# Transfers issued by ScalarE, smaller rings, a moved bias table and norm sums, and 14 U steps through HBM in a one-core transformer layer

## The chip, the cores and the metric

The kernel runs on one core of a Trainium2 chip. The metric is device time in microseconds (us) from the start to the end of one execution. An execution is also profiled: the profile gives, for each engine, when each instruction ran and what it waited for. TensorE multiplies matrices, VectorE and ScalarE work on tiles in on-chip memory, GpSimd does simple vector work and issues the indirect row gathers, and SyncE issues transfers. Each engine works through its own list of instructions in order.

## The reference, cut to what matters

One layer of a streaming encoder over 640 rows of width 2048: 512 new prompt frames (four tiles of 128) and 128 sample frames (one tile).

```
def layer(x, ...):
    z = rmsnorm(x, norm_mix_g) @ w_in
    q, k, v, u, vs, ga, gb = split_in(z, sgu_norm_g)
    o = attend(q, k, v, rel_bias(table), mask, sinks)     # sliding window, grouped heads
    s = sgu(u, vs, w_s, b_s)                              # gated mixing over 128 frames
    h = x + merge(o, s, ga, gb, w_branch_attn, w_branch_sgu, w_out)
    return h + peer(rmsnorm(h, norm_ffn_g))

def peer_tokens(xt, w_query, sub_keys, expert_u, expert_v):
    s = einsum('thpd,hpnd->thpn', query(xt), sub_keys)    # 8 heads, 2 halves, 128 keys
    sv, si = top_k(s, 16);  cv, ci = top_k(all sums of pairs, 16)
    eidx = the 16 * 8 expert numbers of the token, out of 16384
    a = gelu(expert_u[eidx] . xt)
    return sum(softmax(cv) * a * expert_v[eidx])
```

The result is the layer's output after a last norm, with the new rows of K, V and of the gated branch.

## The kernel before

The tokens go through in two groups. G1 is tile 0 and the sample; G2 is tiles 1, 2 and 3. The order in time is: the input projections, attention and gated branch of G1 ("mix"), G1's query with the search for the best experts, the mix of G2, the query of G2, a weights stage, and then the dense experts.

All large products run in `gemm` (lines 192 to 218). It loads two rows of weight blocks (`raw`, 512 KB, a ring of 4), splits each block into a high half (`whi`, a ScalarE cast, line 143) and a low half (`wlo`, a subtraction, line 144, on VectorE), both in rings of 5, and issues three products per tile (lines 211 to 213). After each pair of blocks `pump` advances a list of side generators (`side`: attention, gated branch, search, lookups, one-hots) by a pace of `steps[0]`, and `tick` advances the background gather (`bg`).

The experts are applied in two ways. For G1 `gather_peer` fetches 128 rows of U and 128 of V per token by indirect DMA (two tiles, 512 steps of 1 MB), and VectorE does a dot product (line 740) or an accumulation (line 745) on each. For G2 all experts are computed densely. `weights` builds a 128 x 16384 matrix of gates for each tile from one-hots (lines 782 to 799) and writes it to HBM (`wd`). U step s (`U`, 32 of them) gives 512 activations per token through a gelu (line 829); the first LEAD of them go to HBM as `ad` (line 831), since the gates aren't there yet. `h_step` loads the gates (line 813), multiplies them by the activations (line 814), transposes the product (line 818) and splits it into HT, which `V` (16 blocks of four column parts) multiplies by the V weights and adds to y. `late` does the same for the steps whose activations went to HBM and loads them first. `LEAD` also says which blocks of V run before a U step: from block LEAD/2 - 1 on, the two U steps for the next block come between the parts of V.

`prep` brings the input tiles: x pieces of four blocks, times the norm's gain, split into halves; then the sums of squares, for which ScalarE reads xn (line 435). For G1 it runs in the start, driven by `start_rows`; for G2 it is a side generator `nextg`, eight steps of which `first` lets run in the second branch of the mix of G1, four more in G1's query, and the rest behind those. `bias_table` (lines 222 to 233) computes a table of relative position biases and writes it to HBM (`bvd`), from where the attention loads it. `sample_consts` (lines 312 to 332) loads the caches for the sample.

What sets the order: the kernel's code is a Python program that emits instructions; a scheduler then places each on its engine's list by readiness and priority, so an edit moves instructions far from it. Each transfer that SyncE or ScalarE issues is counted by one of eight counters, taken in turn, and it waits until the counter's previous transfer has landed. SyncE issues nearly all transfers, GpSimd the gathers.

The lines that the prediction's steps touch:

```
    w = load(wd[G[i]][:, s * 512:s * 512 + 512])          # 813, SyncE
    nc.vector.tensor_mul(w, w, a)                          # 814
    ...
    nc.sync.dma_start(ad[s][i], a)                         # 831, SyncE
    ...
    x1 = load(x1d[i][:, nb * 512:nb * 512 + 512])          # V, b == 0
    nc.vector.tensor_add(y[i, nb], x1, ps)                 # 847
```

Of the kernel before, what the change touches and what calls it, by code (L numbers as in the profile page):

```python
# [18 lines left out]
D = 2048  # L19
KC = 16  # L20
# [5 lines left out]
LEAD = 12  # L26
RATE_A = 1.35
# [5 lines left out]
SW = 1.6  # L33
# [9 lines left out]
D_STAGE = 5  # L43
D_LOAD = 4
# [15 lines left out]
def body(tc, A, O):  # L60
    nc = tc.nc
    with ExitStack() as ctx:
# [34 lines left out]
        def load(src, shape=(128, 512)):  # L97
            t = pools["wk"].tile(list(shape), F32, name=nm("b"), tag="b", bufs=cfg["b"])
            nc.sync.dma_start(t, src)
            return t  # L100
# [211 lines left out]
        def sample_consts(vnat, out):  # L312
            vnd = dr.tile([128, 128], F32, name="vnd")
            nc.sync.dma_start(vnd, vnat)
            yield
            kc = mtile([128, 2, 8, 128])
            nc.vector.memset(kc, 0.0)
            for kv in range(2):
                nc.sync.dma_start(kc[kv * 64:kv * 64 + 64, kv], A["kcT"][kv * 64:kv * 64 + 64])
            vc = mtile([128, 8, 128])  # L320
            nc.sync.dma_start(vc, A["vc"])
            sk = stat(2)
            nc.sync.dma_start(sk, A["sinks_s"])
# [5 lines left out]
            vn = mtile([16, 8, 128])  # L329
            nc.sync.dma_start(vn, vnd.rearrange("(b t) d -> t b d", b=8))  # L330
            out.extend((kc, vc, vn, sk, bias))
            yield
# [86 lines left out]
        def prep(G, xgT, r1, order):  # L419
            for i, c in order:  # L420
                if c == 0:
                    xgT.append((mtile([128, KC, 128], F32R), mtile([128, KC, 128], F32R)))
                xh, xl = xgT[i]
                k = slice(4 * c, 4 * c + 4)
                x = stage((128, 4, 128))
                nc.sync.dma_start(x, A["xT"][G[i]][:, k, :])
                (nc.vector if len(G) == 2 and c + i == 0 else nc.gpsimd).tensor_mul(
                    x, x, gmix[:, k].unsqueeze(2).to_broadcast([128, 4, 128]))
                split(xh[:, k, :], xl[:, k, :], x)
                yield  # L430
            for i, ti in enumerate(G):
                s4 = stat(5)
                for c in range(4):
                    xn = load(A["xn"][ti][:, c * 512:c * 512 + 512])
                    nc.scalar.activation(xn, xn, AF.Square, accum_out=s4[:, c:c + 1])
                nc.vector.tensor_reduce(s4[:, 4:5], s4[:, 0:4], axis=AX.X, op=ALU.add)
                r1.append(rstd(s4[:, 4:5], D, "r1"))
                yield
# [4 lines left out]
        def mix(G, xgT, r1, ticks, pre=None):  # L443
# [90 lines left out]
            if n == 2:  # L534
                side.append(first(nextg, EARLY))
# [239 lines left out]
        def weights(ti, ijg):  # L775
# [7 lines left out]
            for t0 in range(0, 128, 4):  # L783
# [15 lines left out]
                nc.sync.dma_start(wd[ti][t0:t0 + 4, :].rearrange("t (i j) -> i t j", i=128), w)  # L799
                yield  # L800

        def dense_peer(G, x2T, r2, x1d):
            n = len(G)
            ad = [[dr.tile([128, 512], F32, name=nm("ad")) for _ in G] for _ in range(LEAD)]
            if True:
# [3 lines left out]
                def h_step(s, i, a):  # L809
                    b, hf = divmod(s, 2)  # L810
                    if (b, i) not in HT:
                        HT[b, i] = mtile([128, 2, 8, 128], F32R)
                    w = load(wd[G[i]][:, s * 512:s * 512 + 512])
                    nc.vector.tensor_mul(w, w, a)  # L814
                    yield
# [19 lines left out]

                def late(s):
                    for i in range(n):
                        a = load(ad[s][i])
                        yield from h_step(s, i, a)

                def V(b, nb, ticks):
                    def ev(i, ps):
                        x1 = y.get((i, nb))
                        if b == 0:
                            x1 = load(x1d[i][:, nb * 512:nb * 512 + 512])
                            y[i, nb] = slot()
                        nc.vector.tensor_add(y[i, nb], x1, ps)  # L847
                        if b == 15:
# [8 lines left out]
                gf = {}  # L857
                steps[0] = SW
# [9 lines left out]
                open_work("d")  # L868
                steps[0] = 1.0
# [30 lines left out]
        side.append(bias_table())  # L900

        def start_rows(kc):
# [3 lines left out]
            if kc == 6:  # L906
                side.insert(0, start)
# [106 lines left out]
```

## Time and profile before

| what | value |
|---|---|
| median of 3 runs | 3991.54 us (3985.18 to 3993.43) |
| the profiled execution | 3996.57 us, of which the span of instructions 3994.9 us |
| TensorE busy | 3883.8 us, 97% |
| VectorE busy | 3153.5 us, 79% |
| ScalarE busy | 1728.2 us, 43% |
| GpSimd busy | 829.1 us, 21% |
| moved by DMA | 1180.5 MB, 296 GB/s in the mean |

The shares are averages over stages with different limits; which wait counts is read from each stage. The stages by time: mix of G1 to 562 us, its query to about 700, mix of G2 to 1510, its query to 1757, the weights stage to 2206, the dense experts to 3976, then the last norm. In the trace a row names the line, the engine and the tiles (out<-in); the time in brackets is how long the engine was idle before, with what released it. PE is TensorE, PEld its weight loads, DVE VectorE, ACT ScalarE, POOL GpSimd, SP SyncE. The clock is the share of full speed that TensorE was granted; full speed is 2.4 GHz and 0.50 is 1.2 GHz. Lines are those of the kernel before.

### The profile page before, as it was taken

What the parts mean: (1) busy time and instruction counts of PE and PEld (TensorE: products, weight loads), DVE (VectorE), ACT (ScalarE), POOL (GpSimd) and SP (SyncE); (2) the same over time, 40 slices, a digit from 0 to 9 for tenths busy, and PEclk for the clock granted to TensorE, in tenths of its full rate; (3) what the DMA queues carried; (4) which work ended last, traced back from release to release, by engine and by line L of the source; (5) the groups of instructions that cost most, each with busy time, mean ns of one, the idle gap of its engine ahead of it and who ended that gap; (6) DMA issues with size and microseconds to landing.
All of it is one profiled execution on the core that took longest, in us unless ns stands there. A gap on an engine that the chain in (4) does not pass through costs nothing. (4 is left out here: it accounts for less than half of the span.)

```text
span 3994.9 us, 52665 instructions
## 1 busy us (share of the span) xinstructions
PE 3883.8 (97%) x17880; PEld 3177.5 (80%) x17880; DVE 3153.5 (79%) x5421; ACT 1728.2 (43%) x3338; POOL 829.1 (21%) x678
## 2 busy tenths in 40 slices
PE   8999998999999999999999899999999999999998
PEld 6778786877777888877878788877888888888886
DVE  4655769966767987899977688878888888888888
ACT  5665554444444334436665333333333333333333
POOL 1000113211212223211111112222222222222222
PEclk9999999999999999999999999999999999999999
DMA  7666786777878997569988989989998999999987
GB/s 224 204 187 208 248 264 201 273 276 279 311 277 286 336 334 249 206 198 314 327 264 288 338 325 338 342 299 365 338 350 336 353 331 345 345 340 349 346 337 290
DMA packets 333919, 1180.51 MB, mean 296 GB/s; under 512 B 35840, under 2 KB 94784, under 8 KB 267088
## 3 DMA queue, kind: packets, MB, share of 16 engines
q1 hardware_dynamic: 259824, 640.15, 47.9%
q0 software_dynamic: 73824, 536.99, 35.0%
q8 instruction: 141, 2.31, 0.2%
q14 instruction: 130, 1.06, 0.1%
HBM read 1117.69 MB, written 59.31 MB: 295 GB/s over the span
## 5 line engine op out<-in xcount | busy, mean ns | idle before, releaser
L211 PE MATMUL acc<-whi,m 128*128 128x512 f32 (+1 forms) x5232 | 2066.7, 395 | 23.3 <-ACT whi L143 18.3
L212 PE MATMUL acc<-wlo,m 128*128 128x512 f32 (+1 forms) x5232 | 2049.8, 392 | 22.5 <-DVE wlo L144 22.4
L213 PE MATMUL acc<-whi,m 128*128 128x512 f32 (+1 forms) x5232 | 2044.1, 391 | 0.3 <-DVE m L144 0.2
L143 ACT CAST whi<-raw 128x512 fp32r<-128x512 f32 (+1 forms) x1888 | 1157.9, 617 | 1979.3 <-PE acc L213 1646.6
L144 DVE TENSOR_TENSOR wlo<-raw,whi 128x512 fp32r<-128x512 f32 (+1 forms) x1824 | 1221.5, 689 | 526.8 <-ACT whi L143 523.1
L212 PEld LDWEIGHTS acc<-wlo,m 128*128 128x128 f32 x5232 | 990.7, 189 | 227.1 <-DVE wlo L144 34.5
L211 PEld LDWEIGHTS acc<-whi,m 128*128 128x128 f32 x5232 | 989.3, 189 | 225.4 <-ACT whi L143 20.6
L213 PEld LDWEIGHTS acc<-whi,m 128*128 128x128 f32 x5232 | 989.5, 189 | 202.7 <-DVE m L144 0.8
L740 DVE SCALAR_TENSOR_TENSOR gb<-gb,xa 128x2048 f32<-128x2048 f32 x256 | 589.6, 2303 | 79.5 <-DMA gb<-in_U,idx 69.1
L745 DVE SCALAR_TENSOR_TENSOR xa<-gb,hw,xa 128x2048 f32<-128x2048 f32 x239 | 560.3, 2344 | 70.4 <-DMA gb<-in_V,idx 64.1
L754 POOL DMA_INDIRECT gb<-in_V,idx x239 | 318.5, 1333 | 1228.8 <-DVE wlo L144 331.2
L754 POOL DMA_INDIRECT gb<-in_U,idx x256 | 339.6, 1327 | 1018.9 <-ACT whi L143 366.2
L144 POOL TENSOR_TENSOR wlo<-raw,whi 128x512 fp32r<-128x512 f32 x64 | 91.5, 1431 | 261.8 <-ACT whi L143 229.7
L796 PEld LDWEIGHTS pm<-s 128*128 128x128 f32 x768 | 102.6, 193 | 30.5 <-ACT s L793 14.6
L796 PE MATMUL pm<-s 128*128 128x128 f32 x768 | 113.7, 283 | 10.0 <-DVE s L789 8.0
L789 DVE TENSOR_SCALAR s<-io,S 128x128 f32<-128x128 f32 x384 | 114.8, 339 | 3.6 <-DMA wd<-s 3.6
L847 DVE TENSOR_TENSOR s<-s,acc 128x512 f32<-128x512 f32 x180 | 112.5, 678 | 0.0
L144 DVE TENSOR_TENSOR m<-pm,m 128x512 fp32r<-128x512 f32 (+1 forms) x142 | 93.5, 661 | 7.5 <-ACT m L143 6.5
L143 ACT CAST m<-pm 128x512 fp32r<-128x512 f32 (+1 forms) x142 | 79.6, 563 | 16.3 <-PE pm L362 6.3
L798 ACT COPY s<-pm 128x512 f32<-128x512 f32 x96 | 56.5, 588 | 64.8 <-PE pm L796 64.2
L814 DVE TENSOR_TENSOR b<-b,b 128x512 f32<-128x512 f32 x36 | 24.8, 688 | 56.0 <-DMA b<-wd 53.5
L792 ACT ACTIVATE s<-io,S 128x128 f32<-128x128 f32 x192 | 66.7, 398 | 3.6 <-DVE S L782 2.3
(194 smaller groups left out, 1668.7 us busy)
## 6 DMA issues: line engine op xcount, KB each, us to landing
raw<-in_UT SPq DMA_DIRECT2D x256, 512.0 KB, 6.2
raw<-in_VP SPq DMA_DIRECT2D x256, 512.0 KB, 6.5
raw<-in_w_in SPq DMA_DIRECT2D x224, 512.0 KB, 4.6
raw<-in_w_out SPq DMA_DIRECT2D x64, 512.0 KB, 5.4
raw<-in_w_q SPq DMA_DIRECT2D x64, 512.0 KB, 4.5
wd<-s SPq DMA_DIRECT2D x96, 256.0 KB, 6.0
b<-wd SPq DMA_DIRECT2D x96, 256.0 KB, 5.2
raw<-in_w_pa SPq DMA_DIRECT2D x32, 512.0 KB, 4.2
```

Of the source, the lines that this page charges most:

```text
L143: mark[0] = nc.scalar.copy(hi, src).ins
L144: (E or nc.vector).tensor_sub(lo, src, hi.bitcast(F32))
L211: nc.tensor.matmul(o, xh, hi, start=(k == 0), stop=False)
L212: nc.tensor.matmul(o, xh, lo, start=False, stop=False)
L213: nc.tensor.matmul(o, xl, hi, start=False, stop=(k == K - 1))
L740: q = nc.vector.scalar_tensor_tensor(t, t, 1.0, xg, op0=ALU.mult, op1=ALU.mult, accum_out=dots[:, j:j + 1])
L745: q = nc.vector.scalar_tensor_tensor(y, t, hw[:, j:j + 1], y, op0=ALU.mult, op1=ALU.add)
L754: d = nc.gpsimd.indirect_dma_start(out=t, out_offset=None, in_=src, in_offset=bass.IndirectOffsetOnAxis(ap=idx[j // 32][:, j % 32:j % 32 + ...
L789: nc.vector.tensor_scalar(a, io128, tr[:, 0, t:t + 1], tr[:, 2, t:t + 1], op0=ALU.is_equal, op1=ALU.mult)
L792: nc.scalar.activation(b, io128, AF.Abs, bias=tr[:, 3, t:t + 1])
L796: nc.tensor.matmul(pw[:, t - t0, :], a, b, start=True, stop=True)
L847: nc.vector.tensor_add(y[i, nb], x1, ps)
```

## The change

The pace constants: the mixing stage asks for more gather steps (RATE_A 1.35 to 1.6), and the weights stage for fewer work steps per pair of blocks (SW 1.6 to 1.35). LEAD goes from 12 to 14. In the dense stage the ring of staging tiles S shrinks from 5 to 3, that of loaded tiles b from 4 to 3, and a new ring h of 3 takes the activations that come back from HBM.

The stores of gates (96) and of activations (now 42) and the loads of both are issued by ScalarE (`E=nc.scalar`). `h_step` issues its loads one step before its multiply and takes its HT tile after it, and `late` issues the next tile's loads before this tile's transposes. The y tiles are loaded from HBM by SyncE before the first block's products, and no longer through the ring b.

`bias_table` is advanced after the start's norm sums; it began before the first product. `sample_consts` clears a tile on GpSimd, and has three more pauses. For G2 `prep` does its sums of squares before the x pieces, and three more steps of it run ahead in the mix of G1.

```diff
-LEAD = 12
-RATE_A = 1.35
+LEAD = 14
+RATE_A = 1.6
-SW = 1.6
+SW = 1.35
-D_STAGE = 5
-D_LOAD = 4
+D_STAGE = 3
+D_LOAD = 3
+D_ACT = 3
-        def load(src, shape=(128, 512)):
-            t = pools["wk"].tile(list(shape), F32, name=nm("b"), tag="b", bufs=cfg["b"])
-            nc.sync.dma_start(t, src)
+        def load(src, shape=(128, 512), tag="b", E=None):
+            t = pools["wk"].tile(list(shape), F32, name=nm(tag), tag=tag, bufs=cfg["b"] if tag == "b" else D_ACT)
+            (E or nc.sync).dma_start(t, src)
@@ bias_table
-            for _ in range(5):
+            for _ in range(3):
                 yield
@@ sample_consts
+            vn = mtile([16, 8, 128])
+            nc.sync.dma_start(vn, vnd.rearrange("(b t) d -> t b d", b=8))
+            sk = stat(2)
+            nc.sync.dma_start(sk, A["sinks_s"])
             kc = mtile([128, 2, 8, 128])
-            nc.vector.memset(kc, 0.0)
+            nc.gpsimd.memset(kc, 0.0)
             for kv in range(2):
                 nc.sync.dma_start(kc[kv * 64:kv * 64 + 64, kv], A["kcT"][kv * 64:kv * 64 + 64])
+                yield
             vc = mtile([128, 8, 128])
             nc.sync.dma_start(vc, A["vc"])
+            yield
@@ prep: rows() and sums() hold the two old loops
+            for part in (sums, rows) if len(G) == 3 else (rows, sums):
+                yield from part()
@@ mix
             if n == 2:
-                side.append(first(nextg, EARLY))
+                side.append(first(nextg, 3 + EARLY))
@@ weights
-                nc.sync.dma_start(wd[ti][t0:t0 + 4, :].rearrange("t (i j) -> i t j", i=128), w)
+                nc.scalar.dma_start(wd[ti][t0:t0 + 4, :].rearrange("t (i j) -> i t j", i=128), w)
@@ h_step
+                    if a is None:
+                        a = load(ad[s][i], tag="h" if opened[0] else "b", E=nc.scalar)
+                    w = load(wd[G[i]][:, s * 512:s * 512 + 512], E=nc.scalar)
+                    yield
+                    nc.vector.tensor_mul(w, w, a)
+                    yield
                     if (b, i) not in HT:
                         HT[b, i] = mtile([128, 2, 8, 128], F32R)
-                    w = load(wd[G[i]][:, s * 512:s * 512 + 512])
-                    nc.vector.tensor_mul(w, w, a)
-                    yield
@@ U
-                            nc.sync.dma_start(ad[s][i], a)
+                            nc.scalar.dma_start(ad[s][i], a)
@@ late
+                    gens = [h_step(s, i, None) for i in range(n)]
+                    next(gens[0])
                     for i in range(n):
-                        a = load(ad[s][i])
-                        yield from h_step(s, i, a)
+                        next(gens[i])
+                        if i + 1 < n:
+                            next(gens[i + 1])
+                        yield
+                        for _ in gens[i]:
+                            yield
@@ V
-                        x1 = y.get((i, nb))
-                        if b == 0:
-                            x1 = load(x1d[i][:, nb * 512:nb * 512 + 512])
-                            y[i, nb] = slot()
-                        nc.vector.tensor_add(y[i, nb], x1, ps)
+                        nc.vector.tensor_add(y[i, nb], y[i, nb], ps)
@@ V, before its gemm
+                    if b == 0:
+                        for i in range(n):
+                            y[i, nb] = slot()
+                            nc.sync.dma_start(y[i, nb], x1d[i][:, nb * 512:nb * 512 + 512])
@@ the start
-        side.append(bias_table())
             if kc == 6:
-                side.insert(0, start)
+                side.extend([start, bias_table()])
```

Three places show how instructions move. The numbers behind names tell tiles apart, and they differ between the two kernels.

The first place is SyncE's list in the start. Before, the bias table's loads (e) and its write (bvd) stood among the x pieces (S<-in_xT):

```order
L224 DMA e_177<-in_table 32x16
L226 DMA e_179<-in_onehot 32x384
L198 DMA raw_186<-in_w_kv 128x512
L426 DMA S_188<-in_xT 128x512
L426 DMA S_193<-in_xT 128x512
L198 DMA raw_218<-in_w_kv 128x512
L198 DMA raw_240<-in_w_kv 128x512
L231 DMA bvd<-e_183 512x1x384
L426 DMA S_242<-in_xT 128x512
L426 DMA S_247<-in_xT 128x512
```

and now the same stretch reads:

```order
L199 DMA raw_177<-in_w_kv 128x512
L430 DMA S_179<-in_xT 128x512
L430 DMA S_184<-in_xT 128x512
L199 DMA raw_209<-in_w_kv 128x512
L430 DMA S_233<-in_xT 128x512
L199 DMA raw_231<-in_w_kv 128x512
L430 DMA S_238<-in_xT 128x512
L199 DMA raw_263<-in_w_kv 128x512
L430 DMA S_287<-in_xT 128x512
L100 DMA b_339<-in_xn 128x512
```

The table's two loads and its write are gone from there, and the x pieces stand between the raw loads one by one; the bias table follows after the loads of xn.

The second place is where a tile's gates (wd) are complete in the weights stage and the first load of them (b<-wd) is issued. Before, this was on SyncE, together with the loads of U weights (raw):

```order
L799 DMA wd_16498<-s_17664 128x4x128
L799 DMA wd_16498<-s_17684 128x4x128
L198 DMA raw_18067<-in_UT 128x1024
L799 DMA wd_16498<-s_17735 128x4x128
L198 DMA raw_18138<-in_UT 128x1024
L99 DMA b_20317<-wd_16498 128x512
L99 DMA b_20358<-ad_15232 128x512
```

Now it is on ScalarE, among the one-hots (L801, L802), the copies out of the accumulators (L807) and the casts:

```order
L790 COPY S_18076<-pm_18072 128x384
L807 COPY s_18040<-pm_18023 128x512
L808 DMA wd_16673<-s_18040 128x4x128
L801 ACTIVATE s_18080<-io_82,S_18076 128x128 x2
L802 ACTIVATE s_18080<-s_18080 128x128 x2
L144 CAST whi_18248<-raw_18233 128x512
L100 DMA b_20872<-wd_16673 128x512
L807 COPY s_18096<-pm_18079 128x512
L801 ACTIVATE s_18131<-io_82,S_18076 128x128
```

The store of the gates and the load behind it now stand ahead of ScalarE's next copy and cast, one copy and one cast apart.

The third place is the passage from the last U step of the weights stage to the first V block. Before, ScalarE went from the last three gelus straight to the casts of the first V weights:

```order
L829 ACTIVATE S_20702<-acc_20417,stats 128x512
L829 ACTIVATE S_20705<-acc_20418,stats 128x512
L829 ACTIVATE S_20708<-acc_20419,stats 128x512
L143 CAST whi_20724<-raw_20722 128x512
L143 CAST whi_20737<-raw_20722 128x512
```

Now ScalarE issues two more stores of activations, then activation loads (h<-ad) and gate loads (b<-wd), and the casts follow:

```order
L843 DMA ad_15319<-S_21261 128x512
L843 DMA ad_15320<-S_21264 128x512
L100 DMA h_21312<-ad_15285 128x512
L100 DMA b_21314<-wd_16673 128x512
L100 DMA h_21317<-ad_15286 128x512
L100 DMA b_21319<-wd_18071 128x512
L100 DMA h_21389<-ad_15287 128x512
L100 DMA b_21391<-wd_19472 128x512
L100 DMA h_21540<-ad_15288 128x512
L144 CAST m_21349<-pm_21350 128x512
L144 CAST whi_21286<-raw_21284 128x512
L144 CAST whi_21299<-raw_21284 128x512
```

Seven loads and the split of the first product (m) now come before the first cast of V weights on ScalarE; three of the loads belong to each of two rings of three, and the seventh is the fourth of ring h. On SyncE, three loads of y (s<-x1d) are now ahead of the first V weights.

## Rows read from the trace of the kernel before

**Rows 1.** The page's first part: busy us of each engine, share of the span.

```profile
PE 3883.8 (97%) x17880; PEld 3177.5 (80%) x17880; DVE 3153.5 (79%) x5421; ACT 1728.2 (43%) x3338; POOL 829.1 (21%) x678
```

**Rows 2.** Waits of TensorE, whole span: total us, times, longest.

```profile
PE acc L212 <- DVE wlo L144: 22.4, 18, 4.8
PE acc L211 <- ACT whi L143: 18.3, 5, 7.4
PE pm L598 <- ACT e L595: 13.1, 3, 5.7
PE pm L796 <- DVE s L789: 8.0, 1, 8.0
PE pm L779 <- DVE S L676: 7.1, 1, 7.1
PE pm L818 <- DVE b L814: 4.6, 2, 3.3
```

**Rows 3.** Stretches: length, busy us of PE, PEld, DVE, ACT, POOL, clock, DMA.

```profile
0.00:62.00 62.00, 42.74 (x181) 34.52 (x182) 29.84 (x55) 30.72 (x70) 10.38 (x16) 0.89 0.81 236
562.00:700.00 138.00, 120.97 (x557) 98.22 (x556) 114.64 (x418) 71.22 (x139) 51.01 (x38) 0.95 0.68 221
1222.00:1371.00 149.00, 142.54 (x672) 117.51 (x671) 119.65 (x176) 60.44 (x101) 29.62 (x26) 1.00 0.86 310
1757.00:2206.00 449.00, 426.35 (x2202) 354.01 (x2202) 386.27 (x865) 265.70 (x675) 58.30 (x48) 0.97 0.84 280
2210.30:2217.10 6.80, 4.75 (x11) 3.45 (x12) 4.78 (x6) 3.42 (x6) 1.35 (x1) 0.50 1.02 398
```

**Rows 4.** Waits of TensorE in the start, 0 to 62 us.

```profile
PE acc L211 <- ACT whi L143: 11.4, 3, 7.4
PE acc L211 <- ACT m L143: 5.0, 1, 5.0
```

**Rows 5.** SyncE's timeline at the start: start, length, what it issues.

```profile
10.88 0.70 SPq L231 DMA_DIRECT2D bvd<-e  x1
11.62 4.74 SPq L426 DMA_DIRECT2D S<-in_xT  x2
```

**Rows 6.** GpSimd's timeline at the start; in brackets its idle time and releaser.

```profile
21.33 2.03 POOL L427 TENSOR_TENSOR S<-S,gmix 128x512 f32<-128x512 f32 x2 [10.04 <-DMA S<-in_xT]
```

**Rows 7.** Waits of ScalarE in the first query, 562 to 700 us.

```profile
ACT b L435 <- DMA b<-in_xn: 18.3, 9, 3.8
ACT stats L137 <- DVE stats L436: 7.5, 2, 5.7
```

**Rows 8.** VectorE's timeline in the weights stage, near 2042 us.

```profile
2049.20 0.69 DVE L814 TENSOR_TENSOR b<-b,b 128x512 f32<-128x512 f32 x1 [8.68 <-DMA b<-wd]
```

**Rows 9.** SyncE's timeline there, two issues that follow each other.

```profile
2035.26 0.46 SPq L198 DMA_DIRECT2D raw<-in_UT  x1
2043.18 0.33 SPq L99 DMA_DIRECT2D b<-wd  x1
```

**Rows 10.** SyncE's timeline at the passage from U to V.

```profile
2205.38 1.68 SPq L831 DMA_DIRECT2D ad<-S  x3
2207.22 0.34 SPq L198 DMA_DIRECT2D raw<-in_VP  x1
```

**Rows 11.** ScalarE's timeline at the passage from U to V.

```profile
2211.67 1.14 ACT L143 CAST whi<-raw 128x512 fp32r<-128x512 f32 x2 [4.97 <-DMA raw<-in_VP]
```

**Rows 12.** VectorE's timeline at the switch from tile 0 to the sample.

```profile
2678.23 2.29 DVE L740 SCALAR_TENSOR_TENSOR gb<-gb,xa 128x2048 f32<-128x2048 f32 x1 [7.66 <-DMA xa<-xgd]
```

**Rows 13.** DMA issues, whole span: count, KB each, median us to landing.

```profile
wd<-s SPq DMA_DIRECT2D x96, 256.0 KB, 6.0
b<-wd SPq DMA_DIRECT2D x96, 256.0 KB, 5.2
ad<-S SPq DMA_DIRECT2D x36, 256.0 KB, 5.6
```

**Rows 14.** VectorE's timeline in the tail.

```profile
3978.40 2.35 DVE L726 SCALAR_TENSOR_TENSOR xa<-xa,stats,m 128x2048 f32<-128x2048 f32 x1 [0.39 <-DMA m<-in_gfin]
```

More of the change, by code (lines that the diff above doesn't have):

```diff
@@ L315, in sample_consts @@
             yield
+            vn = mtile([16, 8, 128])
+            nc.sync.dma_start(vn, vnd.rearrange("(b t) d -> t b d", b=8))
+            sk = stat(2)
+            nc.sync.dma_start(sk, A["sinks_s"])
             kc = mtile([128, 2, 8, 128])
-            nc.vector.memset(kc, 0.0)
+            nc.gpsimd.memset(kc, 0.0)
             for kv in range(2):
                 nc.sync.dma_start(kc[kv * 64:kv * 64 + 64, kv], A["kcT"][kv * 64:kv * 64 + 64])
+                yield
             vc = mtile([128, 8, 128])
             nc.sync.dma_start(vc, A["vc"])
-            sk = stat(2)
-            nc.sync.dma_start(sk, A["sinks_s"])
+            yield
             bias = slot((128, 2, 144))
@@ L328, in sample_consts @@
                                           ap=[[32 * 384, 8], [383, 16], [1, 144]]))
-            vn = mtile([16, 8, 128])
-            nc.sync.dma_start(vn, vnd.rearrange("(b t) d -> t b d", b=8))
             out.extend((kc, vc, vn, sk, bias))
@@ L419, in prep, with rows, sums @@
         def prep(G, xgT, r1, order):
[L420 to L429, printed above, removed]
-                yield
[L431 to L438, printed above, removed]
+            def rows():
+                for i, c in order:
+                    if c == 0:
+                        xgT.append((mtile([128, KC, 128], F32R), mtile([128, KC, 128], F32R)))
+                    xh, xl = xgT[i]
+                    k = slice(4 * c, 4 * c + 4)
+                    x = stage((128, 4, 128))
+                    nc.sync.dma_start(x, A["xT"][G[i]][:, k, :])
+                    (nc.vector if len(G) == 2 and c + i == 0 else nc.gpsimd).tensor_mul(
+                        x, x, gmix[:, k].unsqueeze(2).to_broadcast([128, 4, 128]))
+                    split(xh[:, k, :], xl[:, k, :], x)
+                    yield
+            def sums():
+                for i, ti in enumerate(G):
+                    s4 = stat(5)
+                    for c in range(4):
+                        xn = load(A["xn"][ti][:, c * 512:c * 512 + 512])
+                        nc.scalar.activation(xn, xn, AF.Square, accum_out=s4[:, c:c + 1])
+                    nc.vector.tensor_reduce(s4[:, 4:5], s4[:, 0:4], axis=AX.X, op=ALU.add)
+                    r1.append(rstd(s4[:, 4:5], D, "r1"))
+                    yield
+            for part in (sums, rows) if len(G) == 3 else (rows, sums):
+                yield from part()
         sinks = const.tile([128, 8, 2], F32, name="sinks")
@@ L810, in h_step @@
                     b, hf = divmod(s, 2)
+                    if a is None:
[4 more added lines that the diff above has]
+                    yield
                     if (b, i) not in HT:
                         HT[b, i] = mtile([128, 2, 8, 128], F32R)
-                    w = load(wd[G[i]][:, s * 512:s * 512 + 512])
-                    nc.vector.tensor_mul(w, w, a)
-                    yield
                     pt = misc((128, 4, 128))
@@ L836, in late @@
                 def late(s):
+                    gens = [h_step(s, i, None) for i in range(n)]
+                    next(gens[0])
                     for i in range(n):
-                        a = load(ad[s][i])
-                        yield from h_step(s, i, a)
+                        next(gens[i])
+                        if i + 1 < n:
+                            next(gens[i + 1])
+                        yield
+                        for _ in gens[i]:
+                            yield
                 def V(b, nb, ticks):
                     def ev(i, ps):
-                        x1 = y.get((i, nb))
-                        if b == 0:
-                            x1 = load(x1d[i][:, nb * 512:nb * 512 + 512])
-                            y[i, nb] = slot()
-                        nc.vector.tensor_add(y[i, nb], x1, ps)
+                        nc.vector.tensor_add(y[i, nb], y[i, nb], ps)
                         if b == 15:
@@ L857, in dense_peer @@
                 gf = {}
+                opened = [False]
                 steps[0] = SW
@@ L868, in dense_peer @@
                 open_work("d")
+                opened[0] = True
                 steps[0] = 1.0
```

## The prediction

> **What bounds the kernel now.** I read the page's shares first: TensorE is busy 97% of a span of 3994.9 us [rows 1]. So its idle time is about all there is to win: 3994.9 - 3883.8 = 111 us, a part of which is the end, after the last product. Then I asked whom TensorE waited for [rows 2]: no wait is large; VectorE's low halves (wlo), ScalarE's high halves (whi), the query's evictions, a one-hot, an index lookup and a multiply each cost 5 to 22 us in all. Third, the stretches [rows 3]: the losses lie in the start, the first query and the weights stage, while 1222 to 1371 us has 142.5 of 149 busy. A wait costs more than its length: after one, the first products run at the lower clock level. Behind the stop that ends at 2212 us the granted clock is 0.50 for 6.8 us [rows 3], which costs half of that, 3.4; the mean is 0.89 in the start, 0.95 in the query and 0.97 in the weights stage. I count 3.4 us behind a stop of 5 us or more, and half of that, 1.7, behind a shorter one.
>
> **The change part by part.** The sum is made against the profiled execution, 3996.6 us.
>
> Start. SyncE issues the bias table's write (bvd) at 10.88 us, having waited for the table's product and its copy, and the x pieces only behind it, at 11.62 [rows 5]; GpSimd stood 10.0 us for them [rows 6] and TensorE 5.0 [rows 4]. Now table, product and write come behind the first norm sums (first order piece). That stop and 3.4 at the lower clock can go. The cache loads for the sample, which came in one burst, are spread over several steps: of TensorE's 11.4 us on whi, 7.4 is the first load of all and 4.0 are later stops [rows 4], with 1.7 of clock. At most 5.0 + 3.4 + 4.0 + 1.7 = 14; the x pieces still share the queue with raw loads that wait for buffers. I take -10 (-14 to -3).
>
> First query. ScalarE sat 18.3 us on loads of xn for the next tiles' norms and 7.5 in a square root that waited for VectorE [rows 7]. Behind it stood the query's evictions; TensorE lost two stops there, 10.9 of its 13.1 us on them [rows 2], with 2 x 3.4 of clock: 17.7 in all. But VectorE has 114.6 of 138 us in the stage [rows 3], so I take -8 (-17 to 0). The 12 loads and squares go into the second branch of the mix before it, where ScalarE can wait for them in the same way; there VectorE has no routing to do, and the casts in store cover most. +2 (0 to +7).
>
> Gather rate 1.6 in the second mix: some 16 more steps there, each 2.3 us of VectorE [rows 12], 37 us over 810. Its tightest part has 149 - 119.7 = 29 us of VectorE free [rows 3] and takes two or three of them. +3 (0 to +10). Later stages have these steps less, which is worth nothing where TensorE has no wait.
>
> Weights stage: now 14 steps of U with 1.35 work steps per raw pair for 12 with 1.6 (14 x 8 x 1.35 = 151 for 154), so the one-hots spread over a sixth more time. The longest stop, 8.0 us on a one-hot [rows 2], came from VectorE, which sat 8.7 us in a multiply until b<-wd had landed [rows 8]. That load now comes a step ahead of its multiply: -8, and -3.4 of clock. But it can't start before the last store of its tile has landed, 6.0 us [rows 13], and now it stands on ScalarE ahead of the next copies and casts (second order piece). TensorE then has 24 products and 4 one-hots ahead, by 672 in 142.5 us [rows 3] 28 x 0.21 = 5.9 us, and needs a copy or cast of 0.6 and an issue or two of 0.4 behind the load: each of three tiles stops it 1.5 to 3.5 us, +8, and 3 x 1.1 of clock. Net 0 (-8 to +8). The lookup, 7.1 us [rows 2], keeps its groups and their order: 0 (-5 to +5).
>
> Issues. 96 stores and 96 loads of weights, 42 stores and 42 loads of activations go to ScalarE: 276 of about 0.4 us [rows 9], 110 us more on an engine that is busy 266 of 449 us in the weights stage [rows 3] and less later. As busy time its own idle time covers this: 0; without that cover it would be the whole 110. The trace shows no place in steady state where SyncE's time to issue held TensorE: whi waited there for TensorE, not for raw. The Trainium skill, "DMA: Bandwidth & Descriptors", section "Issuing engines are not separate DMA queues", says that starting transfers from several engines saves only the time it takes to start them. Rows 10 and 11 agree: the raw tile was issued behind 1.68 us of stores and its landing took the rest of the stop. By that rule the move gains nothing but 1.7 us here; by the sum below it gains nothing.
>
> The passage from U to V. Before, SyncE issued three ad stores from 2205.38 to 2207.06 and the first V raw at 2207.22 [rows 10]; ScalarE waited 5.0 us and began to split it at 2211.67 [rows 11], 4.5 after its issue; TensorE stood 6.4 of its 18.3 us on whi [rows 2]. Now SyncE issues three y loads first, and each transfer waits for the previous holder of its completion counter, which for this raw is an ad store. ScalarE issues the stores, three pairs of loads and a fourth activation load before it splits that raw (third order piece). Stores issued until 2207.6 land 5.6 later [rows 13], 2213.2; the raw 4.5 later, 2217.7; a cast, 0.6: TensorE restarts at 2218 to 2220 for 2212.3. By the other path: a pair issued at 2208 lands at 2214, multiply 0.7, a ring of three frees, transposes 1.1, two casts 1.2: 2217. I take +8 (+4 to +13), some clock in the upper end.
>
> First V blocks. TensorE lost 4.6 us on multiplies that waited for b<-wd [rows 2], with 1.7 of clock. The loads are now one step earlier, and the next one is issued ahead of this one's transposes: -5 (-6 to 0). In blocks 0 to 5, 36 loads of activations stand on ScalarE in order, each till the multiply of three loads before has freed its place. In the order that multiply's own load was issued about three casts earlier, some 6 us, so little is left to wait, with four or five casts in store of 9 x 0.21 = 1.9 us each: +3 (0 to +15).
>
> Gather. The switch from tile 0 to the sample put a stop of 7.7 us on VectorE [rows 12] while a step of U ran; TensorE lost 6.6 of its 22.4 us on wlo around it [rows 2]. Now it falls a step of U later, into V products of the next block, where fewer gather steps are due: -4 (-10 to +3). The last steps come ten earlier, so the gather's last scaling of 2.35 us, which stands between TensorE's end and the closing sums [rows 14], leaves the tail: -2.5 (-3 to -1).
>
> Sum: -10 - 8 + 2 + 3 + 0 + 0 + 0 + 8 - 5 + 3 - 4 - 2.5 = -13.5, so 3983 for an execution like the profiled one. That lies 5.1 above the median of three, 3991.5; the median becomes 3978.
>
> **The rivals.** Slower: ScalarE blocked in order. A load that waits for a landing or a ring place holds every cast behind it. A load lands 5.2 us after its issue [rows 13] and its multiply may stand behind a dot product: 5.2 + 2.3 + 0.7 = 8.2. With five casts in store TensorE has 9.5 us and loses nothing; with three it has 5.7 and loses 2.5, and 1.7 of clock. It decides from the point where a load comes to ScalarE's head under 2.5 us after the one three before. If one in six of the 36 meets that and the weights stage's stops come at their upper end, 6 x 4.2 + 8 = 33 instead of 3: +16.5, 4008; with one in three +42, 4033. For it: SyncE issued b<-wd at 2043.18, 7.5 us after the end of the issue before it [rows 9], and the raw load behind came only then. Against: in the V blocks ScalarE waits mostly for TensorE. The Trainium skill, "PSUM — Partial Sum Buffer", section "Engine vs sequencer instructions", calls ScalarE's queue strictly first in, first out; rows 9 agree for SyncE, and the rule makes this case possible at the same price.
>
> VectorE sets the pace. ScalarE's waits only hid VectorE's: the query gives 0, the switch 0, the start 5 less. -13.5 + 8 + 4 + 5 = +3.5: 3995. For it: 114.6 of 138 us in the query [rows 3]; against: the two long stops there end with a ScalarE eviction.
>
> The change misses its mark: the 18.3 us of waits for xn cost the second branch two stops as they cost the query (+13 for +2), and the x pieces are held by raw buffers as before (-3 for -10): -13.5 + 11 + 7 = +4.5: 3996. For it: ScalarE stands in order there too; against: the second branch has no chain of evictions and routing.
>
> **How the numbers follow.** Forecast 0.52 (its own range 3966 to 3988); VectorE 0.15; missed mark 0.13; ScalarE blocked 0.20. Less than 0.2%, 8 us, can't be told from no change. Of the forecast 0.45 lies under 3983.5, of the two middle cases 0.08, of the blocked case 0.02: faster 0.55. Over 3999.5 lie 0.15 of the blocked case and 0.06 of the middle ones: slower 0.21; same 0.24. The range reaches from 3960 to 4008, the smaller price of the blocked case.
>
> **What would show it.** Start: x pieces issued before 11 us, no stop of 5 us before 30. Query: no wait for xn, TensorE's stops under 5 us in all. Weights: three stops of 1.5 to 3.5 us that end with ScalarE's copy or cast, none of 8. Passage: a stop of 12 to 16 us with the V raw landing late. Blocks 0 to 5: TensorE's waits for whi under 5 us in all. End: no L726 behind the last product. I am wrong if ScalarE stands over 8 us in loads again and again in the V blocks, or if the query's stops stay, under VectorE's name.

## The result and the profile after

The changed kernel takes 4024.39 us (4014.85 to 4027.53); the kernel before took 3991.55. The ratio is 1.0080 (1.0063 to 1.0097): slower, where 13.5 us faster was forecast. A second sitting gave 4023.68, ratio 1.0095 (1.0077 to 1.0113). The profiled execution took 4027.53 us, span 4025.8.

TensorE is busy for about as long as before (3891.5 us for 3883.8), and most of the loss is idle time. Its waits, as in [rows 2], whole span:

```profile
PE acc L213 <- DVE wlo L145: 59.7, 34, 5.9
PE acc L212 <- ACT whi L144: 15.6, 5, 7.5
PE pm L830 <- DVE b L824: 13.5, 2, 10.8
PE pm L788 <- DVE S L685: 6.5, 1, 6.5
PE pm L805 <- DVE s L798: 5.2, 2, 3.8
```

VectorE's low halves cost 59.7 for 22.4 us, the multiply 13.5 for 4.6; the query's eviction (L598 before) is gone. By the first product of each stage in the two traces, a stage lasts (us):

| stage | before | after | without ScalarE's transfers (a_sync) | start alone (b_start) |
|---|---|---|---|---|
| start, w_in of G1 | 377.3 | 373.7 | 372.4 | 373.6 |
| second branch of G1 | 49.2 | 53.4 | 53.0 | 48.2 |
| query of G1 | 120.3 | 119.0 | 117.1 | 119.9 |
| w_in of G2 | 547.1 | 551.1 | 554.1 | 545.3 |
| second branch, output of G2 | 206.6 | 220.7 | 220.0 | 206.5 |
| U 0 to 13, V 0 and 1 | 744.4 | 749.3 | 728.8 | 733.2 |
| V 2 to 5 | 281.2 | 291.8 | 289.5 | 285.0 |
| the rest of U and V | 1272.2 | 1274.7 | 1275.0 | 1278.3 |

Stages left out agree within 1.5 us, but for the end (below). Each column is one execution. The profiled execution of before was a long one, and its U row is 11 us over that of b_start (profiled in its longest execution, 3989.57), whose U and V work is the same; against that the changed kernel loses 16 us there.

**Start.** The stretches after (columns as in [rows 3]: length, busy us of PE, PEld, DVE, ACT, POOL, clock, DMA) for the start, the first query, and the weights stage up to the first V product:

```profile
0.00:62.00 62.00, 43.52 (x198) 34.01 (x199) 29.53 (x53) 30.28 (x70) 13.88 (x17) 0.94 0.80 229
562.00:700.00 138.00, 122.73 (x563) 97.20 (x562) 116.56 (x417) 63.98 (x112) 52.48 (x38) 0.98 0.62 204
1786.00:2303.00 517.00, 481.29 (x2438) 403.78 (x2437) 425.31 (x903) 295.14 (x708) 70.43 (x56) 0.96 0.85 282
```

The last x piece was issued at 12.04 us, before at 19.95 [rows 5 has the pair at 11.62]. TensorE's stop of 5.0 is gone, but two others came at the start of the next block, the first of w_in:

```profile
28.11 0.73 PE L212 MATMUL acc<-whi,m 128*128 128x512 f32 x2 [3.03 <-ACT whi L144]
...
31.88 0.73 PE L212 MATMUL acc<-whi,m 128*128 128x512 f32 x2 [1.87 <-ACT whi L144]
```

ScalarE had the norm sums and the next casts in one list there. The first product's stage became 7.5 us shorter and the next block of w_in 4.2 longer.

**First query.** TensorE's two longest waits between 562 and 700 us, before and then in the changed kernel:

```profile
PE pm L598 <- ACT e L595: 10.9, 2, 5.7
PE acc L212 <- DVE wlo L144: 5.4, 5, 2.0
```

```profile
PE acc L213 <- DVE wlo L145: 14.1, 8, 3.7
PE acc L213 <- DVE s L634: 0.6, 1, 0.6
```

ScalarE no longer waits for xn there. Its two stops of 10.9 us are gone, but the waits for VectorE grew from 5.4 to 14.1, so that the stage is only 1.3 us shorter.

**Weights stage.** ScalarE's two longest waits from 1786 to 2320 us in the changed kernel:

```profile
ACT s L807 <- PE pm L805: 90.0, 85, 5.0
ACT whi L144 <- PE acc L214: 74.6, 65, 10.2
```

and from 1770 to 2300 us in the kernel with the same transfers on SyncE:

```profile
ACT whi L144 <- PE acc L214: 145.3, 132, 9.3
ACT s L807 <- PE pm L805: 46.0, 86, 1.3
```

The wait for TensorE (acc) can be read as ScalarE's lead over it: how long a cast stood ready to go but for a place. It was 145 us over 132 casts, and with ScalarE's transfers it is 75 over 65, so less is left to cover the next delay. But the copies of the gates (L807) waited 44 us longer for TensorE in the same stretch, and no run splits how much of that was lead too; that the lost lead made the loss is argued, not shown.

Against a_sync the changed kernel loses 6.5 us in U 4 (51.1 for 44.6), 4.4 in U 6, where the first load of gates stands, and 7.9 in U 13 with the passage. In U 4 VectorE's list has two accumulations of the gather (L754) one behind the other. The second stood for its gathered row, the one-hots (L798) behind it stood too, and TensorE stopped:

```profile
1861.95 2.35 DVE L754 SCALAR_TENSOR_TENSOR xa<-gb,hw,xa 128x2048 f32<-128x2048 f32 x1 [4.41 <-DMA gb<-in_V,idx]
```

```profile
1864.71 1.62 PE L805 MATMUL pm<-s 128*128 128x128 f32 x6 [3.77 <-DVE s L798]
```

In a_sync there are one-hots and low halves between the two, and neither engine stands. U 4 takes 50.2 to 51.1 us in each of the six kernels with 14 steps whose gate stores ScalarE issues, and 44.6 or 44.7 where SyncE does (a_sync, a_store, c14): this loss belongs to the stores, by way of the order on another engine. The first load of a tile's gates shows the hold in ScalarE's own rows:

```profile
1980.89 0.37 ACTq L808 DMA_DIRECT2D wd<-s  x1
...
1986.67 0.34 ACTq L100 DMA_DIRECT2D b<-wd  x1
1987.05 0.59 ACT L807 COPY s<-pm 128x512 f32<-128x512 f32 x1 [4.09 <-DMA wd<-s]
```

The copy and the casts behind it stood 4.09 us for the landing of the tile's last store, and TensorE 1.8; at the second tile it was 3.16 and 0.7, and the third shows no such stop.

**Passage from U to V.** ScalarE, then TensorE, from the last gelu; times in brackets as before:

```profile
2292.65 0.91 ACTq L843 DMA_DIRECT2D ad<-S  x2
2293.60 0.47 ACTq L100 DMA_DIRECT2D h<-ad  x1
...
2296.79 0.99 ACTq L100 DMA_DIRECT2D h<-ad  x1
2301.98 0.33 ACTq L100 DMA_DIRECT2D b<-wd  x1
2302.87 0.33 ACTq L100 DMA_DIRECT2D h<-ad  x1
2304.11 0.59 ACT L144 CAST m<-pm 128x512 fp32r<-128x512 f32 x1 [10.90 <-DMA h<-ad]
2304.59 1.14 ACT L144 CAST whi<-raw 128x512 fp32r<-128x512 f32 x2
```

```profile
2302.99 1.08 PE L830 MATMUL pm<-ident,b 128*128 128x128 f32 x4 [10.82 <-DVE b L824]
...
2306.72 1.09 PE L830 MATMUL pm<-ident,b 128*128 128x128 f32 x4 [2.66 <-DVE b L824]
```

The seventh load (2302.87) stood until the first multiply, as in the forecast's second path; whi followed at 2304.59, right behind the split m and not behind a landing of its raw tile. TensorE stood 10.82 and 2.66, 13.5 for 6.4 before. From the last U product to the first V product it took 15.7 us, for 6.8 before and 9.6 in a_sync.

**V blocks 2 to 5.** ScalarE's waits over the whole span for two releasers:

```profile
ACT whi L144 <- DVE b L824: 84.7, 17, 9.9
...
ACT gb L732 <- DVE xa L754: 11.1, 1, 11.1
```

The first is the ring of three: a load of activations waits for the multiply, and the cast behind it waits too (17 times, up to 9.9). TensorE waited for no high half (whi) from 2310 to 2769 us, so the casts in store covered these waits. The second is one event at the end of tile 0's gather: the square of its result stands in ScalarE's list and waits for the last accumulation, and casts behind it wait 11 us. ScalarE, then TensorE:

```profile
2581.21 0.63 ACT L144 CAST whi<-raw 128x512 fp32r<-128x512 f32 x1 [1.42 <-PE acc L214]
2592.97 1.91 ACT L732 ACTIVATE gb<-xa 128x2048 f32<-128x2048 f32 x1 [11.14 <-DVE xa L754]
```

```profile
2595.39 0.79 PE L213 MATMUL acc<-wlo,m 128*128 128x512 f32 x1 [5.89 <-DVE wlo L145]
```

**End.** VectorE after the last product, to be compared with [rows 14]:

```profile
4009.93 2.05 DVE L862 TENSOR_TENSOR s<-s,acc 128x512 f32<-128x512 f32 x3 [9.48 <-PE acc L214]
4011.89 1.89 DVE L868 TENSOR_TENSOR s<-s,b 128x512 f32<-128x512 f32 x3
4013.70 0.28 DVE L904 TENSOR_REDUCE stats<-stats 128x1 f32<-128x4 f32 x3
```

No L726 (now L735) stands there: 14.6 us from the last product to the end, 18.2 before. This end depends on both pace constants, as a_rate135 shows.

### The profile page after: what moved, and what is told of

Its sections match the earlier page's. It is cut to its first block, busy times and chain, and to the rows that moved or that the text cites. A ratio compares the mean times of both kernels' runs of the same rounds, so it can differ in the third digit from the quotient of the medians.

```text
span 4025.8 us, 52516 instructions
## 1 busy us (share of the span) xinstructions
PE 3891.5 (97%) x17880; PEld 3182.3 (79%) x17880; DVE 3154.1 (78%) x5420; ACT 1730.1 (43%) x3338; POOL 835.4 (21%) x679
## 4 chain that ended last, share of the span: by engine, by line
PE 68%; DVE 13%; DMA 12%; issue 5%; ACT 1%; SPq 0%; ACTq 0%; POOL 0%; DVEq 0%; POOLq 0%
PE acc L213 21%; PE acc L214 21%; PE acc L212 21%; DMA gb<-in_U,idx 6%; DVE wlo L145 3%; DVE gb L749 2%; PE pm L805 2%; DMA gb<-in_V,idx 2%; DVE xa L754 1%; PE pm L830 1%; PE pm L306 1%; DMA wd<-s 1%; DVE S L633 1%; DMA raw<-in_w_out 1%; PE pm L287 0%
## 5 line engine op out<-in xcount | busy, mean ns | idle before, releaser
L213 PE MATMUL acc<-wlo,m 128*128 128x512 f32 (+1 forms) x5232 | 2056.1, 393 | 60.3 <-DVE wlo L145 59.7
L754 DVE SCALAR_TENSOR_TENSOR xa<-gb,hw,xa 128x2048 f32<-128x2048 f32 x249 | 591.1, 2374 | 85.8 <-DMA gb<-in_V,idx 70.7
L763 POOL DMA_INDIRECT gb<-in_V,idx x249 | 344.1, 1382 | 1253.6 <-DVE wlo L145 390.7
L805 PEld LDWEIGHTS pm<-s 128*128 128x128 f32 x768 | 114.9, 192 | 27.8 <-issue 6.0
L862 DVE TENSOR_TENSOR s<-s,acc 128x512 f32<-128x512 f32 x192 | 120.7, 680 | 9.5 <-PE acc L214 9.5
L798 DVE TENSOR_SCALAR s<-io,S 128x128 f32<-128x128 f32 x384 | 115.6, 342 | 4.4 <-DMA wd<-s 4.4
L807 ACT COPY s<-pm 128x512 f32<-128x512 f32 x96 | 56.4, 588 | 97.6 <-PE pm L805 90.0
L144 ACT CAST m<-pm 128x512 fp32r<-128x512 f32 (+1 forms) x142 | 79.8, 564 | 33.8 <-DMA h<-ad 10.9
L801 ACT ACTIVATE s<-io,S 128x128 f32<-128x128 f32 x192 | 75.7, 396 | 1.3 <-DVE s L804 0.5
L830 PE MATMUL pm<-ident,b 128*128 128x128 f32 x384 | 58.8, 276 | 13.5 <-DVE b L824 13.5
```

The costliest lines, as they stand in the source:

```text
L144: mark[0] = nc.scalar.copy(hi, src).ins
L213: nc.tensor.matmul(o, xh, lo, start=False, stop=False)
L754: q = nc.vector.scalar_tensor_tensor(y, t, hw[:, j:j + 1], y, op0=ALU.mult, op1=ALU.add)
L763: d = nc.gpsimd.indirect_dma_start(out=t, out_offset=None, in_=src, in_offset=bass.IndirectOffsetOnAxis(ap=idx[j // 32][:, j % 32:j % 32 + ...
L798: nc.vector.tensor_scalar(a, io128, tr[:, 0, t:t + 1], tr[:, 2, t:t + 1], op0=ALU.is_equal, op1=ALU.mult)
L805: nc.tensor.matmul(pw[:, t - t0, :], a, b, start=True, stop=True)
```

## The experiments

Times are medians; ratios are to the kernel before in the same sitting. The `a_` kernels undo a part of the change, the `b_` kernels do one part alone.

**a_rate135**, `-RATE_A = 1.6` `+RATE_A = 1.35` on the changed kernel. 

> The changed kernel with RATE_A back at 1.35. Theory 1 (gather pace): the 16 extra gather steps in the second mix cost the time there (w_in +4.0, second branch +4.8, output product +9.3 us in the two traces) and move the switch of gather tiles into V blocks 2 to 5 (+10.6): 20 to 28 us come back, to about 4000, and those four parts return to within 2 us of before. Theory 2 (ScalarE blocked in order): the losses lie in its transfers; the V blocks keep +8 or more, only the mix returns, and it gains 8 to 15, to about 4012.

4026.58, 1.0108 (1.0092 to 1.0123). The median did not move, so neither theory has the time. Theory 1 has the places: in the trace, that of the shortest execution (4012.04), w_in, second branch, output and V 2 to 5 gave back 5.6, 4.8, 9.2 and 14.6 us. The steps not asked for in the mix are asked for behind it: the U steps and V blocks after V 5 took 8.7 more, and the end, from the last product on, 31.2 us for 14.6. VectorE behind the last product, which ended at 3979.1:

```profile
3984.12 2.34 DVE L754 SCALAR_TENSOR_TENSOR xa<-m,hw,xa 128x2048 f32<-128x2048 f32 x1
...
3991.99 4.73 DVE L754 SCALAR_TENSOR_TENSOR xa<-m,hw,xa 128x2048 f32<-128x2048 f32 x2
...
4003.20 2.35 DVE L735 SCALAR_TENSOR_TENSOR xa<-xa,stats,m 128x2048 f32<-128x2048 f32 x1 [3.92 <-DMA m<-in_gfin]
```

Four accumulations and the gather's last scaling stand there. All four kernels with LEAD 14 and RATE_A 1.35 have such an end (a_rate135, a_mix, c14, b_lead: 31.2 to 33.4 us); with 12 steps it is 15.1 to 18.3, and with 14 steps and 1.6 it is 14.6. Where the longer executions lose the rest is not seen.

**b_rate16**, `-RATE_A = 1.35` `+RATE_A = 1.6` on the kernel before. 

> The kernel before with RATE_A 1.6 alone. Theory 1: slower by 15 to 25 us, about 4010, with ScalarE's waits for raw<-in_w_out rising from 9 to over 20 us. Theory 2: slower by 10 to 18 in the mix alone, and V blocks 2 to 5 unchanged.

3992.39, 1.0014 (1.0004 to 1.0024): 6 us, under both theories' figures, although the second branch and the output grew by 13.3 us. ScalarE's waits for raw<-in_w_out did rise, from 9.1 to 30.0.

**a_sync**, all four kinds on SyncE:
```diff
-            (E or nc.sync).dma_start(t, src)
+            nc.sync.dma_start(t, src)
-                nc.scalar.dma_start(wd[ti][t0:t0 + 4, :].rearrange("t (i j) -> i t j", i=128), w)
+                nc.sync.dma_start(wd[ti][t0:t0 + 4, :].rearrange("t (i j) -> i t j", i=128), w)
-                            nc.scalar.dma_start(ad[s][i], a)
+                            nc.sync.dma_start(ad[s][i], a)
```


> The changed kernel with the four kinds of gate and activation transfers issued by SyncE again. Theory 1: V blocks 2 to 5 and the mix stay as they are, the time changes by less than 6 us. Theory 2: ScalarE's 84.7 us of waits for the multiply go, V blocks 2 to 5 lose 8 to 10 us and the passage from U to V 3 to 6: 12 us or more faster, about 4011.

4003.84, 1.0049 (1.0035 to 1.0063): 20 us back by the medians, 15 to 19 by the differences to the kernel before in each sitting. Theory 2 holds in the sum and not in the place: V 2 to 5 gave back 2.3, U 0 to 13 with V 0 and 1 20.5.

**a_sums**, `(rows, sums)` for all groups and `first(nextg, EARLY)`. 

> The changed kernel with the second group's norm sums behind the x pieces again and 8 steps ahead. Both theories: the first group's second branch loses its extra 4.2 us and the query gets its two ScalarE stops back. If the stops were VectorE's in the end (the query was only 1.3 us shorter), the time falls by 2 to 4; if the move paid as forecast (+2 and -8), it rises by 6.

4017.05, 1.0084 (1.0070 to 1.0098): 7 us by the medians, within the interval of the whole change by the ratios. In the trace the second branch became 4.9 us shorter and w_in 5.4, while TensorE's two stops within the query's eviction came back with 9.4.

**a_store** and **a_load**: of a_sync's edits only the two stores', and only the loads'. 

> The changed kernel with only the 138 stores (gates and activations) back on SyncE; ScalarE keeps the 138 loads. All transfers back gave 20 us (4024 to 4004), in the steps U 0 to 13 with V blocks 0 and 1 (749 to 729). Theory A (loads that wait hold ScalarE's casts): little comes back, 4 to 8 us, about 4018. Theory B (the stores among the one-hots delay ScalarE's casts and with them the gathers): 12 to 20 us, about 4008.

4008.01, 1.0059 (1.0047 to 1.0071): 16 us back, 12 to 16 by the differences in each sitting, theory B. 

> The changed kernel with only the loads of gates and activations back on SyncE; ScalarE keeps the stores. Theory A: 12 to 20 us faster, about 4008, the passage from U to V shorter by 4 to 8 and no wait of ScalarE for the multiply. Theory B: 4 to 8 faster, about 4018, and the weights stage stays as it is.

4016.03, 1.0078 (1.0065 to 1.0091): 8 us, 4 to 8 by the same differences. Both cost, the stores more, though ScalarE waits for the loads and not visibly for the stores; U 4 has 44.7 us in a_store and 51.1 in a_load.

**b_act**, the four kinds (264 transfers with LEAD 12) on ScalarE in the kernel before; the gate stores' line is changed in the same way:
```diff
-                w = load(wd[G[i]][:, s * 512:s * 512 + 512])
+                w = load(wd[G[i]][:, s * 512:s * 512 + 512], E=nc.scalar)
-                        a = load(ad[s][i])
+                        a = load(ad[s][i], E=nc.scalar)
-                            nc.sync.dma_start(ad[s][i], a)
+                            nc.scalar.dma_start(ad[s][i], a)
...
```


> The kernel before with these stores and loads on ScalarE and nothing else changed (12 steps, rings of 5 and 4, loads right before their multiply). If the issue by ScalarE costs by itself: 15 to 25 us slower than before, about 4006. If it costs only through the rings of three and the longer weights stage: within 6 us.

4039.16, 1.0131 (1.0116 to 1.0145): 52 us, more than any theory had. From the last pair of U blocks to V the trace has 39.5 us for 10.6 in before.

**b_store** and **b_load**, its halves. 

> The kernel before with only the 96 gate stores and 36 activation stores on ScalarE. All four kinds there cost 52 us (3987 to 4039). If the stores cost in the one-hots, as in the changed kernel (16 us back without them): 12 to 20 us slower, about 4003. If they cost only beside the loads: under 6 us.

4016.85, 1.0081 (1.0068 to 1.0094): 29 us, over the range. 

> The kernel before with only the loads of gates and activations on ScalarE, each right before its multiply. If the cost is the hold of ScalarE's casts until the last store of a tile has landed and until a ring place is free: 30 to 45 us slower, about 4025, with the stop of 35 us between U and V. If it needs ScalarE's own stores: under 15.

4008.38, 1.0048 (1.0035 to 1.0062): 21 us, under it, and without the long stop between U and V (13.2 us from the last pair of U blocks to V, 10.8 in b_start). That stop is the stores': 38.8 us from there to V in b_store. ScalarE's last gate store, the load on SyncE that waits for it, and TensorE:

```profile
2198.13 0.37 ACTq L799 DMA_DIRECT2D wd<-s  x1
```

```profile
2204.29 0.33 SPq L99 DMA_DIRECT2D b<-wd  x1
```

```profile
2211.03 1.09 PE L818 MATMUL pm<-ident,b 128*128 128x128 f32 x4 [12.57 <-DVE b L814]
...
2217.07 1.09 PE L818 MATMUL pm<-ident,b 128*128 128x128 f32 x4 [3.58 <-DVE b L814]
2222.17 1.09 PE L818 MATMUL pm<-ident,b 128*128 128x128 f32 x4 [4.01 <-DVE b L814]
2227.92 1.65 PE L211 MATMUL acc<-whi,m 128*128 128x512 f32 x3 [4.66 <-ACT whi L143]
```

In the order that was built, ScalarE's list has 10 or 11 groups of four one-hots per U step with its stores in it and 12 or 13 without, so 15 of the 96 are left for the last step, 6 of them in its last pair of blocks. Then the load waits 6 us for the last store's landing and four multiplies come one after another, with nothing left to cover them. The changed kernel's 14 steps at 1.35 have room for that; what it pays instead lies in the weights stage and the passage.

**b_start**, the moved bias table and `sample_consts` alone. 

> The kernel before with the moved bias table and the changed cache loads alone. By the two traces the start is 3.6 us shorter for the forecast 10: 3 to 5 us faster, about 3982; by the forecast's step 10 faster, about 3976.

3982.72, 0.9979 (0.9971 to 0.9988), as the traces had it. It is the one version that beats both kernels clearly.

**c14** is the changed kernel with a_sync's, a_sums' and a_rate135's edits; **c12** also has LEAD 12 and SW 1.6. 

> The changed kernel with the transfers on SyncE, the norm sums behind the x pieces and RATE_A 1.35; what is left of the change is the start, LEAD 14 with SW 1.35, the early loads, the preloaded y and the rings of three. If the parts add up (4004 with SyncE's transfers, 7 for the sums, 0 to 6 for the rate): 3991 to 3997. If the passage and V blocks 2 to 5 carry the rest on their own: no better than 3997.

3991.80, 1.0001 (0.9992 to 1.0011): in the range for parts that add up. Its end takes 33.0 us, though, 18 more than the changed kernel's, so what it gives back ahead of the last product is more than the time shows. 

> The same with LEAD 12 and SW 1.6 as before: the start, the early loads, the preloaded y and the rings of three alone. If the early loads are worth their stop of 8 us in U step 8 beside the start's 4: 3974 to 3980, better than both kernels. If VectorE or the one-hots stop there anyway: like the start alone, 3981 to 3985. Over 3990 if the smaller rings cost.

3987.13, 0.9996 (0.9985 to 1.0008): by the medians 2 us under before, for 4 by the start alone. Early loads, preloaded y and rings of three together win nothing that can be seen, and may take back a part of what the start gives.

**b_lead**, LEAD 14 and SW 1.35 alone. 

> The kernel before with LEAD 14 and SW 1.35 alone. If six more activation tiles through HBM and two more late steps cost (the difference between c14 and c12): 5 to 15 us slower, 3992 to 4002. If the thinner one-hots pay for them: 3982 to 3990.

3996.55, 1.0019 (1.0008 to 1.0030): 7.5 us slower, and the trace puts that at the end. Up to the last product it is 8.8 us shorter than before: the thinner one-hots gave U 3, 6 and 8 back 29 us, and U 12 and 13 with their one-hots and the passage, and the blocks from U 14 on, took about as much again. The end takes 33.4 us for 18.2, with five accumulations behind the last product, where a_rate135 has four.

**b_sums**, sums first and 11 steps ahead, alone. 

> The kernel before with only the second group's norm sums moved ahead of the x pieces and 11 steps ahead. By the forecast (-8 in the query, +2 in the second branch): 6 us faster, 3981. By the changed kernel, which became 7 us faster without the move: 4 to 9 us slower, 3991 to 3996, with the 4 us in the first group's second branch and VectorE stops in place of ScalarE's in the query.

3993.36, 1.0016 (1.0006 to 1.0026): 6 us slower. TensorE's longest wait in the query there:

```profile
PE acc L212 <- DVE wlo L144: 15.4, 9, 3.7
```

**a_mix**, a_sums' and a_rate135's edits together, beside the changed kernel itself (a_again, 4023.68). 

> The changed kernel with the norm sums and the rate of the second mix as before, and the transfers still on ScalarE. If the sums and the rate cost as each did alone on the kernel before (6 and 6): 10 to 14 us faster than the changed kernel beside it, about 4011. If what the mix gives back is lost again behind it (the rate alone undone gave nothing): within 5.

4014.26, 1.0068 (1.0053 to 1.0083): 9 us, a little under the sum of the two alone, with an end of 32.8 us for the 14.6 of the changed kernel.

## Why the prediction was wrong

The step that failed is "As busy time its own idle time covers this: 0". It counted ScalarE's idle time over a stage, and much of that idle time was spent ahead of TensorE, as its lead. Undone, the 276 issues gave 15 to 20 us in the changed kernel; on the kernel before, 264 of them cost 52 alone. That the transfers cost this is shown; by what way is shown for single stops (U 4, the loads of gates, the passage) and argued for the rest. The forecast's slow rival had a part of the cause, ScalarE held in order, but it put the place in the V blocks and took the price from waits. ScalarE did stand there 17 times, three of them over the 8 us that the forecast named as a sign of being wrong, but V 2 to 5 gave back only 2.3 us without it; the cost lay in the weights stage and the passage.

At the passage the stop had the forecast size (13.5 us for 12 to 16; the first V product 8.9 us later than before, for +8), but by the second of its two paths: the multiply, the transposes and the split m came last, and not the landing of the V raw. Two of the three stops at the first loads of gates came, with 1.8 and 0.7 us for a forecast of 1.5 to 3.5.

Start: -10, measured -4 to -8 alone. The stop went; its neighbours grew.

Query and norm sums: -8 + 2, measured +6 alone. The query's stops stayed under VectorE's name, the forecast's other sign of being wrong: taking away ScalarE's wait let VectorE's come forward; the rival "VectorE sets the pace" was right here, and the case of moved waits for the second branch's 4 us. In the changed kernel and in b_sums w_in of G2 has a further 4.5 to 5 us in one block (its third), where VectorE waits in order for gathered rows; the block ahead of it is 3 to 4 us shorter than in before and 1 to 2 shorter than in b_start:

```profile
788.67 2.29 DVE L749 SCALAR_TENSOR_TENSOR gb<-gb,xa 128x2048 f32<-128x2048 f32 x1 [4.86 <-DMA gb<-in_U,idx]
...
796.36 2.29 DVE L749 SCALAR_TENSOR_TENSOR gb<-gb,xa 128x2048 f32<-128x2048 f32 x1 [4.18 <-DMA gb<-in_U,idx]
```

That these waits follow from the earlier sums is argued, not shown.

Gather rate: +3, measured +6 alone and nothing when undone alone. Its 13 to 14 us in the second branch and output are there in every trace with 1.6; much of it is won back later. A cost in one stage was forecast as if the steps could be had free elsewhere, but with LEAD 14 and 1.35 some of them stand behind the last product.

Weights stage: the forecast 0 for LEAD and pace was 7.5 alone, but not in this stage: 15.2 us more at the end and 8.8 less ahead of it. In the changed kernel the rate of 1.6 keeps that end away. The stop of 8 us on a one-hot did go (U 8: 43.0 us for 56.9).

Gather switch: -4, measured +7 to +11 (V 2 to 5 with 291.8, for 285.0 in b_start and 281.2 before): the end of tile 0's gather moved among the late steps, and ScalarE waited 11.1 us in it.

First V blocks: -5, measured -4.7 in V 0 and 1 against b_start and -8.4 against the long execution of before (V 1, first quarter: 17.2 us for 22.0). End: -2.5, measured -3.6, which needs the rate of 1.6.

From the kernel before: 15 to 20 (transfers) + 6 (sums) + 6 (rate) + 7.5 (LEAD) - 4 to -8 (start) = 26.5 to 35.5, for a measured 33 to 37. That this comes near is in part luck. The transfers are priced in the changed kernel and the rest on the kernel before, and LEAD's 7.5 lies in an end that the changed kernel doesn't have. Without it the sum is 19 to 28, and what fills the gap wasn't measured by itself.

## What to carry to other kernels

Idle time on an engine that feeds another one can be that engine's lead, and not free room: before work goes there, read how long its instructions stood ready and waited for the consumer alone. A transfer on such an engine puts a landing (4.09 us here) or a ring place (9.9) in front of the next tile's feed; SyncE stood for such landings too (7.5 us in [rows 9]), and with the four kinds on it the changed kernel was 15 to 20 us faster. A stop that ends with one engine's name can belong to the engine behind it: move the wait only where that one has room. And background work that a stage doesn't do is done somewhere: look for it behind the last product before a slower pace is called free.

## What the runs showed that was not expected

Moving an instruction's issue to another engine also changed where the scheduler put its neighbours: 12 or 13 one-hot groups per step became 10 or 11, and 28 of b_store's 29 us came at the passage (38.8 us for 10.6 before) with that order. Changing the rate of the gather back gave 34 us in four stages of the changed kernel's trace and left the median as it was; 16.6 of them went to the end.
